# Four modulation steps in the router's wait, and routing weights by a single f32r pass whose parts ScalarE adds

## The chip, the core and the metric

The kernel runs on one core of a Trainium2 chip. Its engines are TensorE (PE; its weight loads are listed as PEld), VectorE (DVE), ScalarE (ACT), GpSimd (POOL) and SyncE (SP), which issues nearly all DMAs here. The metric is the device time of one launch in microseconds; lower is better.

## The reference

A diffusion backbone of two layers over 256 latent and 256 context tokens of width 1024. Layer 0 mixes tokens by windowed attention, layer 1 by differential attention; a mixture of experts follows each. Layer 0's mixture works on all 512 tokens, layer 1's on the 256 latent ones. What the change touches is the modulation `mod`, one row of 6 x 1024 numbers per layer and token kind, and the weights of the experts:

```python
mod  = (silu(c)     @ mod_w[i] + mod_b[i]).reshape(B, 6, 1, D)
modc = (silu(c_ctx) @ mod_w[i] + mod_b[i]).reshape(6, D)
h = rmsnorm(x, norm_g[i, 0]) * (1 + mod[:, 1]) + mod[:, 0]
...
gsel = argmax(lg); p_grp = max(softmax(lg))          # one of 4 groups
top_p, top_i = top_k(softmax(le_sel), 2)             # two of its 8 experts
wts = p_grp * top_p / sum(top_p)
out[token] += wts * ((silu(u[:, :512]) * u[:, 512:]) @ w_down[e]),  u = h[token] @ w_up[e]
```

## The kernel before

**Loads.** All large weights come through one ordered list, `plan`, in pieces of 512 KB. SP issues them one after another, each into one of 43 slots of SBUF (`Slot`); a slot comes free when its last reader is done, and SP waits at the next load until there is a free one.

**Stages.** Projections of layer 0 to 114 us; windowed attention to 228; output projection to 283; the router of layer 0 to 300.4; its 16 expert pairs to 812; the attention of layer 1 to 1046; its router to 1062; its expert pairs to 1525; the end.

**Modulation steps.** `mod_step` (its products are L370) multiplies a quarter of the rows of a third of `mod_w` by the two condition vectors: four pieces of weights, eight products of 32 x 512 in f32, each two instructions on PE. They add up in one PSUM bank over four steps; the fourth returns `mod_finish`, which copies the sum to SBUF, turns it by four transposes (L385) and adds the biases. Of 12 steps four are done in the projections and eight in the attention, where the loop over units (head pair, part) calls one after the units in `MODS`. The last four give the first third of layer 1's modulation, which nothing in layer 0 reads. In the attention the Tile scheduler orders PE's work, so a step can be split there. A head pair has three units; the third's scores are L760, its transposes L792.

**Router (`moe`).** From the logits DVE finds group, two experts and `Mb`, the table of chosen experts (L1013). PE counts with it (L1018, L1024). DVE makes the places `key`, and from these each pair of experts gets `P`, a matrix of 512 tokens x 128 places that holds ones and zeros, in f32r. Meanwhile `shift` rounds the tokens of tiles 2 and 3 to two f32r parts, `hi` by ACT (L977) and `lo` by DVE (L978). In the first pair a pass over `P` gathers 1/rms (`ri`, L1142, copied by L1143). From the router on PE's order is as written in the code.

**Expert pair.** `gather` for pair p+1 runs inside pair p. `gather_weights` (L1188) multiplies `P` by three columns of `WR` (the weights of both experts and 1/rms; two columns in layer 1 and in the first pair) in f32, two instructions per tile, and DVE copies the columns out of PSUM (L1191 twice, L1193). `half` (L1152) gathers the tokens; its sum is scaled by 1/rms in layer 0 (L1162 on ACT, L1160 on DVE). `P` is turned (L1168). `spread_tokens` (L1198, L1200) turns the gathered tokens. `up` is L1209, `down` L1252, `gate` L1216 to L1218, `combine` L1291 with the residual additions L509 on DVE. The bank group G, of two PSUM banks, serves the weights' sums, the gathered halves and the turned `P` in turn.

Of the kernel before, what the change touches and what calls it, by code (L numbers as in the profile page):

```python
# [36 lines left out]
CAP = 64  # L37
# [7 lines left out]
MODS = range(0, 24, 3)  # L45
# [11 lines left out]
def _hybrid_dit(ctx, tc, a, out):  # L57
# [6 lines left out]
               for c, dt in (("f", F32), ("r", F32R))] for i in range(SLOTS)]  # L64
    const = ctx.enter_context(tc.tile_pool(name="const", bufs=1))
# [238 lines left out]
    ident2 = const.tile([128, 64], F32, name="ident2")  # L304
# [3 lines left out]
    ident_b = const.tile([128, 128], BF, name="ident_b")  # L308
# [10 lines left out]
    for t, op in enumerate((OP.is_gt, OP.is_lt)):  # L319
        m = const.tile([128, 128], BF, name=f"mask_b{t}")  # L320
# [58 lines left out]
    def mod_finish(l, third, halves, hb, acc):  # L379
        h0, nh = halves[0], len(halves)  # L380
        sb = row("q")
        ve.tensor_copy(sb[hb], acc[hb])
        tp = bank("G")
# [449 lines left out]
    tmp.free()  # L833
    rooms.pop().free()
# [21 lines left out]
    class Post:  # L856
        def __init__(self, l, nt, lb=None):
# [23 lines left out]
            homes[l].slot.free()  # L881
# [99 lines left out]

    def moe(l, nt, post, after, finish):
        T = nt * 128
        with tc.manual_schedule(engines=PE):
            lg = post.logits()
        post.shift(2, ge)
# [38 lines left out]
        WR = const.tile([128, nt, NE // 2, 3], F32, name=f"WR{l}", tag="WR")  # L1025
        W = WR[:, :, :, 0:2]
        cmi = const.tile([128, 1], I32, name=f"cmi{l}", tag="cmi")

        def weights():
# [22 lines left out]
            if not unit:  # L1052
                ve.tensor_copy(WR[:, :, :, 2], post.ri.unsqueeze(2).to_broadcast([128, nt, NE // 2]))
        h_slots, tok, unit = post.slots, post.tok, post.nr == 1

        np_ = NE // 2
        prev = st = None
        early_ks = range(0, KT // 2) if T == 512 else ()
        late_ks = range(len(early_ks), KT)
        for p in range(np_):  # L1060
# [17 lines left out]
            if p == IF_AT:  # L1078
# [6 lines left out]
                with tc.If(most > CAP):  # L1085
                    overflow(l, nt, key, W, None if unit else post.ri, tok, [hs_[k // 2].f(2, 512)[:, k % 2] for k in range(KT)])
# [39 lines left out]
    def gather(l, nt, p, key, WR, tok, unit, early=None, between=None, ri=None):  # L1126
# [56 lines left out]

    def gather_weights(P, WR, p, st, n):
        wps = bank("G")
        nt = P.shape[1]
        for t in range(nt):
# [617 lines left out]
```

## Time and profile before

| | us |
|---|---|
| median of 3 runs | 1551.51 (1550.75 to 1552.95) |
| the profiled execution | 1550.44 |
| its span, first to last instruction | 1548.8 |
| PE busy in it | 1458.1 (94%) |
| DVE, ACT, POOL busy | 655.5, 384.6, 184.2 |
| mean granted clock of PE | 0.981 |

Starts are microseconds from the span's begin. A granted clock of 1.00 is 2.4 GHz, of 0.50 is 1.2 GHz. Busy shares are means over stages; each stage has its own limit. "[8.10 <-DVE Mb L1013]" behind an instruction says how long its engine had been idle and which instruction ended that.

### The profile page before, as it was taken

Reading aid. Unit: us, or ns where it says so; the run is one execution under the profiler, and the core shown is the slowest. Engines: PE = TensorE matmul, PEld = TensorE weight load, DVE = VectorE, ACT = ScalarE, POOL = GpSimd, SP = SyncE. Lnnn points to the kernel's source line nnn. Section 1 sums busy time; section 2 is a strip of 40 time slices with the busy share of each in tenths; the row PEclk is TensorE's granted clock in tenths of the full one; section 3 lists DMA queues with packets and bytes.
Section 4 is the critical chain, followed back from the end, with each engine's and each line's share of the span. In section 5 each row is a group of like instructions: output and inputs, shape, how many; then the busy total and the mean of one; then the engine's idle time right before and its main releaser. Section 6 shows DMA issues by size and latency. Waiting matters only on the chain. (4 is left out here: it accounts for less than half of the span.)

```text
span 1548.8 us, 20271 instructions
## 1 busy us (share of the span) xinstructions
PE 1458.1 (94%) x7463; PEld 800.3 (52%) x7463; DVE 655.5 (42%) x1585; ACT 384.6 (25%) x823; POOL 184.2 (12%) x147
## 2 busy tenths in 40 slices
PE   6998999799999999999999899798999899999997
PEld 4765567445444454444545678684434333433444
DVE  3338862424333443333448726863323222322323
ACT  4426653211010011101115235652101010110112
POOL 2314551000000000000006463100000000000000
PEclk9999999899999999999998999999999999999999
DMA  9767225799989999999996532488999999999991
GB/s 330 243 214 273 82 86 187 278 366 401 395 343 393 401 398 398 391 397 403 382 297 229 182 124 71 161 284 304 387 409 409 409 408 409 409 409 409 409 394 68
DMA packets 169695, 485.67 MB, mean 314 GB/s; under 512 B 20825, under 2 KB 41586, under 8 KB 169586
## 3 DMA queue, kind: packets, MB, share of 16 engines
q1 hardware_dynamic: 169088, 483.66, 82.2%
q8 instruction: 63, 1.03, 0.3%
q10 hardware_dynamic: 498, 0.60, 0.1%
q14 instruction: 46, 0.38, 0.1%
HBM read 483.16 MB, written 1.05 MB: 313 GB/s over the span
## 5 line engine op out<-in xcount | busy, mean ns | idle before, releaser
L1209 PE MATMUL ps<-slotf,row 128*64 128x512 f32 x2048 | 449.2, 593 | 2.1 <-DVE row L1200 2.1
L1209 PEld LDWEIGHTS ps<-slotf,row 128*64 128x64 f32 x2048 | 145.2, 137 | 289.7 <-issue 274.4
L1252 PE MATMUL ps<-slotf,row 128*64 128x512 f32 x960 | 212.6, 595 | 0.0
L546 PE MATMUL ps<-slotr,slotr 128*128 128x512 f32 x768 | 193.4, 405 | 13.4 <-DVE slotf L1414 6.7
L509 DVE SCALAR_TENSOR_TENSOR slotf<-ps,mod,slotf 128x256 f32<-128x256 f32 x408 | 167.3, 477 | 62.3 <-PE ps L1291 29.7
L546 PEld LDWEIGHTS ps<-slotr,slotr 128*128 128x128 f32 x768 | 145.1, 194 | 50.4 <-DVE slotf L1414 7.1
L1252 PEld LDWEIGHTS ps<-slotf,row 128*64 128x64 f32 x960 | 66.3, 137 | 124.9 <-issue 118.9
L1216 ACT ACTIVATE row<-ps 128x512 f32<-128x512 f32 x30 | 17.9, 597 | 425.9 <-PE ps L1209 386.6
L1217 DVE SCALAR_TENSOR_TENSOR row<-row,ps 128x512 f32<-128x512 f32 x30 | 20.6, 687 | 234.4 <-ACT row L1216 234.3
L1278 DVE SCALAR_TENSOR_TENSOR row<-ps,ty,row 128x512 fp32r<-128x512 f32 x60 | 45.0, 750 | 176.5 <-ACT row L1277 173.3
L1277 ACT ACTIVATE row<-ps,ty 128x512 fp32r<-128x512 f32 x60 | 41.3, 688 | 263.0 <-PE ps L1252 262.7
L1291 PE MATMUL ps<-row,row 128*128 128x512 f32 (+1 forms) x512 | 104.4, 348 | 1.1 <-DVE slotf L509 1.0
L1291 PEld LDWEIGHTS ps<-row,row 128*128 128x128 f32 x512 | 77.3, 189 | 36.5 <-ACT row L1216 21.1
L521 POOL TENSOR_TENSOR slotr<-slotf,slotr 128x1024 fp32r<-128x1024 f32 x32 | 78.9, 2479 | 86.9 <-ACT slotr L517 72.1
L1200 DVE TENSOR_TENSOR row<-ps,mod 128x512 f32<-128x512 f32 x64 | 42.7, 686 | 101.7 <-PE ps L1198 100.9
L481 POOL TENSOR_TENSOR row<-row,row 128x512 f32<-128x512 f32 (+1 forms) x13 | 15.0, 1156 | 575.6 <-PE ps L1291 519.4
L1152 PE MATMUL ps<-slotf,row 128*128 128x512 f32 x128 | 65.0, 632 | 7.0 <-PEq L1085 4.7
L1152 PE MATMUL ps<-slotr,row 128*128 128x512 f32 x256 | 70.4, 419 | 0.0
L517 ACT ACTIVATE slotr<-slotf 128x1024 fp32r<-128x1024 f32 x44 | 45.9, 1055 | 63.1 <-DMA slotf<-in_diff_w_qkv 38.0
L1152 PEld LDWEIGHTS ps<-slotr,row 128*128 128x128 f32 x256 | 47.9, 198 | 10.0 <-issue 0.8
L1377 PE MATMUL ps<-slotr,slotr 128*128 128x512 f32 x192 | 47.6, 399 | 0.0
L1198 PE MATMUL ps<-ident,row 128*128 128x128 f32 x256 | 37.8, 280 | 7.5 <-DVE row L1156 6.7
(314 smaller groups left out, 1526.8 us busy)
## 6 DMA issues: line engine op xcount, KB each, us to landing
slotf<-in_moe_w_up SPq DMA_DIRECT2D x512, 512.0 KB, 9.5
slotf<-in_moe_w_down SPq DMA_DIRECT2D x256, 512.0 KB, 10.2
slotf<-in_mod_w SPq DMA_DIRECT2D x96, 512.0 KB, 6.3
slotf<-in_diff_w_qkv SPq DMA_DIRECT2D x24, 512.0 KB, 3.9
slotf<-in_win_w_qkv SPq DMA_DIRECT2D x12, 512.0 KB, 5.2
slotf<-in_win_w_o SPq DMA_DIRECT2D x8, 512.0 KB, 4.0
slotf<-in_diff_w_o SPq DMA_DIRECT2D x8, 512.0 KB, 4.1
slotf<-in_x SPq DMA_DIRECT2D x2, 512.0 KB, 4.1
```

What stands on the lines that cost most here:

```text
L509: ve.scalar_tensor_tensor(xT[k][:, sl], ps[:, sl], g[:, k, r:r + 1], xT[k][:, sl], op0=OP.mult, op1=OP.add)
L517: se.activation(hv, v, AF.Copy)
L521: (eng or (ge if split_i[0] % 3 == 0 else ve)).tensor_tensor(lv, v, hv.bitcast(F32), op=OP.subtract)
L546: pe.matmul(ps[t], h[:, x, ts], w[y][:, kk, :], start=(k + kk == 0 and n == 0), stop=(k + kk == KT - 1 and n == 2))
L1152: pe.matmul(g, P[:, t, :] if len(tok[t]) > 1 else P[:, t, :].bitcast(F32), v[:, hs], start=(t == 0 and i == 0), stop=(t == nt - 1 and i == ...
L1200: ve.tensor_tensor(o.rearrange("p (k c) -> p k c", k=4), ps.rearrange("p (k c) -> p k c", k=4), mods[l][:, 3, 4 * h:4 * h + 4, 0:1].to_bro ...
L1209: pe.matmul(u[h][64 * s:64 * s + 64, :], st["xt"][k // 4][:, c0:c0 + 64], w[s][1][:, h * 512:(h + 1) * 512], start=(k == 0), stop=(k == KT ...
L1252: pe.matmul(y[h][64 * s:64 * s + 64, :], acT[:, c0:c0 + 64], w[s][1][:, h * 512:(h + 1) * 512], start=(k == 0), stop=(k == 3))
L1277: se.activation(yh, y[h], AF.Copy, scale=wsl)
L1278: ve.scalar_tensor_tensor(yl, y[h], wsl, yh.bitcast(F32), op0=OP.mult, op1=OP.subtract)
L1291: pe.matmul(out, part[:, c * 128:(c + 1) * 128], st["PT"][:, :T], start=(i == 0), stop=(i == 1))
L1377: pe.matmul(ps, w[x][:, k % 4, ms], oT0[k][1][:, y, :], start=(k == 0 and i == 0), stop=(k == KT - 1 and i == 2))
```

## The change

Three things, all in one file. `MODS` names every sixth unit instead of every third, so four of the eight steps leave the attention. Three of the four are put behind the transposes of layer 0's logits (`mods_meanwhile`); the fourth behind the counts (`last_mods`), its sum copied by ACT and turned after the first gather; the loads of these four steps stand behind those of the output projection. The weights' table `WR` becomes f32r in two parts, hi and lo, and the pass over it f32r by f32r, one instruction per tile over both parts' columns; the parts are added by an ACT copy with an accumulator output (`add_parts`), in place of DVE's copies. The same is done for 1/rms (`rr`). The constants of the attention's masks go into a slot that is freed after it, which pays for the larger `WR`.

```diff
-MODS = range(0, 24, 3)
+MODS = range(0, 24, 6)
...
+    while len(todo) > KT // 2:
+        plan_mod(*todo.pop(0))
+    plan_out(a["win_w_o"][0])
     while todo:
         plan_mod(*todo.pop(0))
-    plan_out(a["win_w_o"][0])
...
-    ident2 = const.tile([128, 64], F32, name="ident2")
+    masks = Slot()
+    ident2 = masks.f()[:, 0:64]
...
+    def mods_meanwhile():
+        while len(mod_steps) > 1:
+            mod_step("A")
+
+    def last_mods():
+        l, third, halves, hb, acc = mod_step("A").args
+
+        def moved():
+            sb = row("q")
+            se.activation(sb[hb], acc[hb], AF.Copy)
+            return partial(mod_turned, l, third, halves, hb, sb)
+
+        return moved
...
             lg = post.logits()
+            mods_meanwhile()
...
-        WR = const.tile([128, nt, NE // 2, 3], F32, name=f"WR{l}", tag="WR")
-        W = WR[:, :, :, 0:2]
+        moved = last_mods() if mod_steps else None
+        cols = 2 if unit else 3
+        WR = const.tile([128, nt, NE // 2, 2, cols], F32R, name=f"WR{l}", tag="WR")
...
+        if not unit:
+            rr = const.tile([128, nt, 2], F32R, name=f"rr{l}")
+            ve.tensor_copy(rr[:, :, 0], post.ri)
+            ve.tensor_tensor(rr[:, :, 1], post.ri, rr[:, :, 0].bitcast(F32), op=OP.subtract)
...
+            hi, lo = WR[:, :, :, 0, :], WR[:, :, :, 1, :]
+            se.activation(hi, wide_w, AF.Copy)
+            ve.tensor_tensor(lo, wide_w, hi.bitcast(F32), op=OP.subtract)
...
+        turn_mods = moved() if moved else lambda: None
...
-                    st = gather(l, nt, 0, key, WR, tok, unit, weights, ri=post.ri)
+                    st = gather(l, nt, 0, key, WR, tok, unit, weights, ri=() if unit else rr)
+                    turn_mods()
...
-                    pe.matmul(wps[:, 0:1], P[:, t, :].bitcast(F32), ri[:, t:t + 1], start=(t == 0), stop=(t == nt - 1))
-                ve.tensor_copy(st["w"][:, 1:2], wps[:, 0:1])
+                    pe.matmul(wps[:, 0:2], P[:, t, :], ri[:, t, :], start=(t == 0), stop=(t == nt - 1))
+                add_parts(st["w"][:, 1:2], wps[:, 0:2])
...
+    def add_parts(dst, src):
+        n = src.shape[0]
+        se.activation(tiny("ap", [128, 2], bufs=2)[:n], src, AF.Copy, accum_out=dst)
+
     def gather_weights(P, WR, p, st, n):
...
+        c = WR.shape[4]
         for t in range(nt):
-            pe.matmul(wps[:, 0:n], P[:, t, :].bitcast(F32), WR[:, t, p, 0:n], start=(t == 0), stop=(t == nt - 1))
+            pe.matmul(wps[:, 0:2 * c], P[:, t, :], WR[:, t, p], start=(t == 0), stop=(t == nt - 1))
+        v = wps[:, 0:2 * c].rearrange("p (b c) -> p c b", b=2)
         for s in range(2):
             pb = slice(64 * s, 64 * s + 64)
-            ve.tensor_copy(st["w"][pb, 0:1], wps[pb, s:s + 1])
+            add_parts(st["w"][pb, 0:1], v[pb, s])
         if n == 3:
-            ve.tensor_copy(st["w"][:, 1:2], wps[:, 2:3])
+            add_parts(st["w"][:, 1:2], v[:, 2])
```

The change adds lines, so a line of before has another number after: L370 is 375, L748 is 756, L749 757, L785 793; in the router and the experts L977 is 987, L1018 1044, L1024 1050, L1142 1182, L1152 1192, L1162 1202, L1168 1208, L1188 1233, L1198 1244, L1200 1246, L1209 1255, L1216 1262, L1217 1263, L1218 1264, L1242 1288, L1291 1337, L509 517.

PE in the attention, from the transposes of a second unit's probabilities to the scores of the next one, before; L370 is the modulation step:

```order
L785 MATMUL ps_1308<-ident,row_1190 128x128 x4
L370 MATMUL ps_1058<-slotf_125,slotf_109 32x512
L785 MATMUL ps_1315<-ident,row_1191 128x128 x4
L370 MATMUL ps_1058<-slotf_127,slotf_109 32x512
L370 MATMUL ps_1058<-slotf_111,slotf_109 32x512
L370 MATMUL ps_1058<-slotf_69,slotf_109 32x512
L370 MATMUL ps_1058<-slotf_125,slotf_109 32x512
L370 MATMUL ps_1058<-slotf_127,slotf_109 32x512
L370 MATMUL ps_1058<-slotf_111,slotf_109 32x512
L370 MATMUL ps_1058<-slotf_69,slotf_109 32x512
L748 MATMUL ps_1334<-slotr_124,slotr_94 128x512 x2
```

The same engine after, in a head pair whose loop calls no step:

```order
L793 MATMUL ps_1481<-ident,row_1363 128x128 x4
L375 MATMUL ps_1097<-slotf_129,slotf_109 32x512
L793 MATMUL ps_1488<-ident,row_1364 128x128 x4
L756 MATMUL ps_1495<-slotr_90,slotr_132 128x512 x2
L757 LDWEIGHTS slotb_169
L757 MATMUL ps_1495<-slotb_169 128x128
```

Where eight products stood in every head pair, this one holds a single product, between the two transposes; the next head pair holds the other seven of the step, two and five.

PE in the router of layer 0 after, from the counts (L1050) to the first gathered half; `ps_2639` is the sum of the moved steps:

```order
L1050 LDWEIGHTS ones_b
L1050 MATMUL ps_2730<-Mb_2715,ones_b 128x32
L375 MATMUL ps_2639<-slotf_75,slotf_109 32x512
...
L375 MATMUL ps_2639<-slotf_67,slotf_109 32x512
L1182 MATMUL ps_2793<-rr_2748,row_2758 128x2 x4
L1192 MATMUL ps_2800<-slotr_120,row_2758 128x512
L1192 MATMUL ps_2800<-slotr_114,row_2758 128x512
```

Before, the pass over `ri` (L1142) followed the counts at once; now seven products of the fourth step (the first and the last are shown) stand between them, and 1/rms is passed in two columns. The fourth step's first product stands ahead of L1044, behind the 24 of the three other steps.

ACT in an expert pair of layer 0, from one pair's last scaling of outputs to the second half of the next gather; before:

```order
L1277 ACTIVATE row_2952<-ps_2923,ty_2728 128x512
L1216 ACTIVATE row_3036<-ps_2957 128x512
L1162 ACTIVATE row_3081<-ps_3072,ty_3063 128x512
L1170 ACTIVATE row_3088<-ps_3083 128x512
L1242 ACTIVATE row_3095<-ps_3090 128x512
```

After:

```order
L1323 ACTIVATE row_3002<-ps_2973,ty_2760 128x512
L1262 ACTIVATE row_3086<-ps_3007 128x512
L1226 ACTIVATE ty_3119,ty_3113<-ps_3114 64x2
L1226 ACTIVATE ty_3121,ty_3113<-ps_3114 64x2
L1226 ACTIVATE ty_3123,ty_3113<-ps_3114 128x2
L1202 ACTIVATE row_3134<-ps_3125,ty_3113 128x512
L1210 ACTIVATE row_3141<-ps_3136 128x512
L1288 ACTIVATE row_3148<-ps_3143 128x512
```

Three additions (L1226), which read the weights' sums `ps_3114`, stand between the gate's activation (L1262) and the scaling of the gathered half (L1202); DVE's two copies are gone from its queue.

## Rows read from the trace of the kernel before

**Rows 1.** Stretches: from:to, length; busy (count) PE, PEld, DVE, ACT, POOL; clock, DMA, GB/s.
```profile
283.00:300.40 17.40, 7.14 (x40) 5.71 (x39) 13.75 (x55) 5.23 (x10) 2.52 (x2) 0.61 0.69 266
300.40:812.00 511.60, 503.71 (x2443) 243.20 (x2444) 190.54 (x425) 61.44 (x102) 2.17 (x2) 0.99 0.98 380
```

**Rows 2.** Stretches: the attention's first one, and one head pair.
```profile
113.70:136.40 22.70, 17.85 (x117) 9.08 (x117) 21.45 (x58) 12.67 (x35) 8.79 (x8) 1.00 0.87 307
172.70:184.60 11.90, 11.90 (x87) 6.94 (x85) 10.74 (x28) 7.35 (x23) 7.18 (x6) 1.00 0.14 45
```

**Rows 3.** Timeline in that head pair: start, us, engine, line, operation, count [idle <-releaser].
```profile
176.38 1.21 PE L760 MATMUL ps<-slotr,slotr 128*128 128x256 f32 x8
179.96 1.04 PE L370 MATMUL ps<-slotf,slotf 128*32 128x512 f32 x2
181.53 1.92 PE L370 MATMUL ps<-slotf,slotf 128*32 128x512 f32 x14
182.09 2.04 POOL L789 TENSOR_TENSOR slotf<-slotf,ty 128x512 f32<-128x512 f32 x2 [2.23 <-DVE ty L770]
184.60 0.82 PE L792 MATMUL ps<-ident,slotf 128*128 128x128 f32 x6
```

**Rows 4.** Timeline of the router, layer 0; then a stretch of it.
```profile
291.02 0.18 PE L1018 MATMUL ps<-Mb,before_b 128*128 128x32 bf16 x1 [8.10 <-DVE Mb L1013]
292.65 1.84 PE L1142 MATMUL ps<-ri,row 128*128 128x1 f32 x8 [1.09 <-DVE s L1031]
293.30 0.63 ACT L977 ACTIVATE slotr<-slotf 128x512 fp32r<-128x512 f32 x1 [2.56 <-DVE slotf L974]
294.35 3.76 PE L1152 MATMUL ps<-slotr,row 128*128 128x512 f32 x8
294.52 0.16 DVE L1143 COPY ty<-ps 128x1 f32<-128x1 f32 x1 [0.99 <-PE ps L1142]
300.38 3.65 PE L1209 MATMUL ps<-slotf,row 128*64 128x512 f32 x16 [0.78 <-DVE row L1200]
...
291.00:298.05 7.05, 5.94 (x31) 4.98 (x31) 5.36 (x19) 1.46 (x4) 0.00 (x0) 0.50 0.40 136
```

**Rows 5.** Timeline of one expert pair of layer 0.
```profile
513.75 2.83 DVE L509 SCALAR_TENSOR_TENSOR slotf<-ps,mod,slotf 128x256 f32<-128x256 f32 x7
513.95 0.95 PE L1188 MATMUL ps<-WR,row 128*128 128x3 f32 x8
514.73 1.69 PEld L1152 LDWEIGHTS ps<-slotr,row 128*128 128x128 f32 x8
514.76 2.09 PE L1152 MATMUL ps<-slotr,row 128*128 128x512 f32 x8
516.83 0.16 DVE L1193 COPY ty<-ps 128x1 f32<-128x1 f32 x1
517.13 0.63 PE L1168 MATMUL ps<-ident,row 128*128 128x128 f32 x4 [0.28 <-DVE ty L1193]
```

**Rows 6.** Waits of PE in layer 0's experts: us, times, longest.
```profile
PE ps L1168 <- DVE ty L1193: 3.7, 13, 0.3
```

**Rows 7.** ACT's instructions by form: count, busy us, mean ns, idle before.
```profile
L768 ACT ACTIVATE ty<-ty 128x2 f32<-128x2 f32 x16 | 3.3, 205 | 0.0
L753 ACT ACTIVATION_READ_ACCUMULATOR row<-ps,ty 128x1 f32 x32 | 6.5, 203 | 0.0
```

**Rows 8.** Timeline of one expert pair of layer 1.
```profile
1265.52 0.50 PE L1188 MATMUL ps<-WR,row 128*128 128x2 f32 x4
1265.72 0.69 DVE L1156 COPY row<-ps 128x512 f32<-128x512 f32 x1 [2.12 <-PE ps L1152]
1266.47 1.09 PE L1198 MATMUL ps<-ident,row 128*128 128x128 f32 x8 [0.45 <-DVE row L1156]
```

**Rows 9.** Stretches: layer 0's steady pairs, layer 1's first pairs.
```profile
481.00:740.00 259.00, 256.69 (x1232) 124.86 (x1233) 98.34 (x220) 30.68 (x49) 0.00 (x0) 0.99 1.00 397
1095.00:1220.00 125.00, 122.86 (x594) 51.79 (x592) 34.14 (x71) 13.35 (x24) 0.00 (x0) 1.00 1.03 409
```

More of the change, by code (lines that the diff above doesn't have):

```diff
@@ L64, in _hybrid_dit @@
                for c, dt in (("f", F32), ("r", F32R))] for i in range(SLOTS)]
+    halves = [nc.alloc_sbuf_tensor_at(f"slotb{i}", [128, 2048], BF, offset=base + 4096 * i).ap() for i in range(SLOTS)]
     const = ctx.enter_context(tc.tile_pool(name="const", bufs=1))
@@ L303, in _hybrid_dit @@
     make_identity(nc, ident)
-    ident2 = const.tile([128, 64], F32, name="ident2")
+    masks = Slot()
+    ident2 = masks.f()[:, 0:64]
+    masks_b = halves[masks.s].rearrange("p (a n) -> p a n", n=128)
     ve.tensor_tensor(ident2, ident[:, 0:64], ident[:, 64:128], op=OP.add)
@@ L307, in _hybrid_dit @@
     ve.memset(ones, 1.0)
-    ident_b = const.tile([128, 128], BF, name="ident_b")
+    ident_b = masks_b[:, 8]
     ve.tensor_copy(ident_b, ident)
@@ L319, in _hybrid_dit @@
     for t, op in enumerate((OP.is_gt, OP.is_lt)):
-        m = const.tile([128, 128], BF, name=f"mask_b{t}")
+        m = masks_b[:, 9 + t]
         ve.tensor_scalar(m, diff_f, 0.0, -BIG, op0=op, op1=OP.mult)
@@ L379, in mod_finish, with mod_turned @@
     def mod_finish(l, third, halves, hb, acc):
-        h0, nh = halves[0], len(halves)
         sb = row("q")
         ve.tensor_copy(sb[hb], acc[hb])
+        mod_turned(l, third, halves, hb, sb)
+    def mod_turned(l, third, halves, hb, sb):
+        h0, nh = halves[0], len(halves)
         tp = bank("G")
@@ L833, in _hybrid_dit @@
     tmp.free()
+    masks.free()
     rooms.pop().free()
@@ L880, in __init__ @@
                 ve.tensor_tensor(self.ws[:, r], wr[l], scl[l][1][:, :, r:r + 1].to_broadcast([128, KT, 36]), op=OP.mult)
-            homes[l].slot.free()
+            if not mod_steps:
+                homes[l].slot.free()
             self.slots = [[Slot() for _ in range(1 if t in WHOLE[l] else 2)] for t in range(nt)]
@@ L1052, in weights @@
             if not unit:
[L1053 to L1054 removed]
+                ve.tensor_copy(wide_w[:, :, :, 2], post.ri.unsqueeze(2).to_broadcast([128, nt, NE // 2]))
+            hi, lo = WR[:, :, :, 0, :], WR[:, :, :, 1, :]
+            se.activation(hi, wide_w, AF.Copy)
+            ve.tensor_tensor(lo, wide_w, hi.bitcast(F32), op=OP.subtract)
+        h_slots, tok = post.slots, post.tok
         np_ = NE // 2
         prev = st = None
+        turn_mods = moved() if moved else lambda: None
         early_ks = range(0, KT // 2) if T == 512 else ()
@@ L1085, in moe @@
                 with tc.If(most > CAP):
-                    overflow(l, nt, key, W, None if unit else post.ri, tok, [hs_[k // 2].f(2, 512)[:, k % 2] for k in range(KT)])
+                    overflow(l, nt, key, WR, None if unit else post.ri, tok, [hs_[k // 2].f(2, 512)[:, k % 2] for k in range(KT)])
                 for s in hs_:
@@ L1090, in moe @@
                 if p == 0:
-                    st = gather(l, nt, 0, key, WR, tok, unit, weights, ri=post.ri)
+                    st = gather(l, nt, 0, key, WR, tok, unit, weights, ri=() if unit else rr)
+                    turn_mods()
+                    if moved:
+                        homes[l].slot.free()
                 if p != IF_AT:
@@ L1318, in overflow @@
         Wov = row("p", (128, nt, NE))
-        ve.scalar_tensor_tensor(Wov.rearrange("p t (a b) -> p t a b", b=2),
-                                key.rearrange("p t (a b) -> p t a b", b=2), float(CAP), W,
+        pairs = Wov.rearrange("p t (a b) -> p t a b", b=2)
+        ve.tensor_tensor(pairs, W[:, :, :, 0, 0:2].bitcast(F32), W[:, :, :, 1, 0:2].bitcast(F32), op=OP.add)
+        ve.scalar_tensor_tensor(pairs, key.rearrange("p t (a b) -> p t a b", b=2), float(CAP), pairs,
                                 op0=OP.is_gt, op1=OP.mult)
```

3 lines of the change are left out of this document (added).

## The prediction

> **What bounds the kernel now.** I read the stages first, then inside each stage the wait that ends last. In the experts of layer 0 TensorE (PE) is busy 503.71 of 511.60 us [rows 1]: an instruction less there is time less, and an idle gap there is time too. The router ahead of them is the opposite: 7.14 busy of 17.40 us. PE stands 8.10 us for `Mb`, the table of chosen experts that VectorE (DVE) makes, and what follows runs at a granted clock of 0.50, the 1.2 GHz level [rows 1, 4]. In the windowed attention a head pair takes 11.90 us with PE busy throughout, while the first stretch is DVE's: 21.45 of 22.70 us against PE's 17.85 [rows 2]. So modulation steps cost PE time in the attention and would find an idle PE in the router; but PE being full in the attention doesn't yet say that its work is what sets the period.
>
> The profiled execution is 1550.44 us, 1.1 under the median of 1551.51. I make the sum on it and add the 1.1.
>
> **Part 1: four steps leave the attention.** A step is 16 instructions of L370. They stand as 2 + 14: from 179.96 to the next start at 180.94 is 0.98 us, and the 14 last 1.85 beyond what they overlap, together 2.83 [rows 3]. Before, the first stretch holds two steps beside the last one of the projections, and each of the six head pairs behind it one. After, by the order of PE, the first stretch keeps one step and one product (of the eight; two instructions) of the next, and the six pairs hold in turn two and five products, one, two and five, one, two and five, none. Two and five cost 0.98 + 1.85 as before, one costs 0.98. So PE is spared 1.85 in the first stretch, 1.85 in two pairs and 2.83 in the last, 8.4 us in all: the most that can be won.
>
> What is late next is the head pair's own chain. The third score (L760) ends at 177.59, and its transposes (L792) start at 184.60: 7.0 us of maximum, exponentials, sum, reciprocal and a multiplication on GpSimd, whose 2.04 us began when DVE's reciprocal L770 let it and waited for nothing of PE [rows 3]. PE fills 2.83 of the 7.0 with the step; with one product it has 5.2 of work there, with none 4.2. The links follow one another on ACT, DVE and GpSimd, so I let a pair with one product shorten by 0.6 and not by 1.85, the pair with none by 1.0, and the first stretch, where DVE is the busier, by 0.8: **−3 us**. Bounds: −8.4 if the chain gives way, 0 if it is rigid.
>
> The new weights' order on the SP queue (the output projection's eight loads before the last four steps' 16) costs nothing: these 16 must wait for slots of the attention either way and then stand ready before the router. The masks now hold a slot until the attention ends, one of 43; 0 to +1, I take 0.
>
> **Part 2: the router takes them.** Three steps, 3 x 1.85 = 5.6 us, stand behind the logits' transposes and inside the 8.10 us in which PE waits for `Mb` [rows 4]: free, and if that cover were gone they would cost their 5.6. The fourth's first product stands with them; its other seven stand after the counts and ahead of the pass that reads 1/rms (L1142 before). PE would reach it at about 291.7 (two DVE operations more in front of `Mb` or behind it, 0.3) and leave it at 293.5 at full clock, 295.4 at half. L1142, eight instructions in 1.84 at half clock, becomes four: 0.9 or less. It ends at about 294.0 to 296.3; before it was 294.49. On ACT two things come between: the copy of the fourth step's sum (about 0.6) and the addition of the 1/rms parts (0.4), and behind them in the queue stands L977, the rounding of the last token tile, which before started at 293.30 [rows 4]. It starts 1.3 to 3 us later, and the second half of L1152 needs it. Against that, L1152 took 3.76 here and 2.09 at full clock [rows 4, 5], and DVE no longer stands 0.99 for L1142 at L1143. The first expert matmul started at 300.38; I get 299.5 with the clock at its upper level and 302.5 to 303 at the lower one, and take **+0.5** (−1 to +3), since three steps leave PE some 2.5 us idle ahead of `Mb` where it had 8.10. Turning the fourth sum (four transposes, five small DVE operations) lies beside the 0.78 us for which PE waits at L1209 anyway.
>
> **Part 3: the weights' pass in layer 0, 15 pairs.** L1188 starts at 513.95 and L1152 behind it at 514.76: 0.81 us for eight instructions of 3 columns, 0.10 each [rows 5]. After: four of 6 columns, single-pass. With so few columns the count sets the price: 0.40, so −0.41. Bounds: L1152's eight weight loads of the same type take 1.69, 0.21 each [rows 5]; at that price four cost 0.85, no gain. Then the wait: L1168 stands 0.28 for L1193, 3.7 us in 13 pairs [rows 6]. PSUM has two banks of this group, L1168 writes the one that the weights' sums are read from, and the copies L1191 and L1193 queue on DVE behind seven residual additions, 2.83 us [rows 5]. Now ACT empties the bank, and in the order nothing stands between its last activation of the pair before and the three additions. Each is an ACTIVATE of two columns and a read of the accumulator: 205 + 203 ns by their nearest rows [rows 7], a = 0.41. They start with the sums at about 514.5, end at 515.7, and L1168 wants the bank at 516.45. So the 0.28 is gone up to a = 0.65, and PE follows at once. 15 x 0.41 + 3.7 = **−9.9** (−3.7 to −11); the first pair's pass, outside these 15, adds **−0.4**.
>
> The rows say that DVE is late here by its queue and not by its price; so I take ACT. The Trainium skill, page "ScalarE: Activation LUTs", section "Rules for kernel authors", says the reverse for the operation as such: additions belong on VectorE. By that rule the 0.28 would stay and the sum would be 3.7 us less, 1542; [rows 5, 6] don't bear it out, the longer instruction stands in an empty queue.
>
> For the f32r weight loads I keep to the rows, 0.10 to 0.21 each. The Trainium skill, page "TensorE: Matmul & The Clock Gate", section "Weight-path perf modes — Fast Weight Load (FWL) and DoubleRow", has weights other than FP32 loaded about twice as fast; by it the pass would be some 0.2 and the sum 3 us lower, an estimate. The f32r loads of L1152 show nothing of that [rows 5].
>
> **Part 4: layer 1, 15 pairs.** Four instructions become two, but the pass lies under another wait: L1198 starts 0.45 after L1188's work, held by the DVE copy L1156 [rows 8]. Gain 0. Two additions on ACT instead of L1191 free the bank at 1265.8 + 2a = 1266.6; the second spread needs it at about 1266.95. **0**, with a loss of 2a − 1.15 a pair beyond a = 0.57; 0 to +2 in all.
>
> **DMA.** At −0.7 a pair layer 0 asks its 24 transfers of 512 KB per 31.07 us, 405 GB/s; it has 397 now and layer 1 shows 409 [rows 9]. It holds, by little: the floor is 30.8 us a pair.
>
> Sum: −3 + 0.5 − 9.9 − 0.4 = −12.8: 1537.6 on the profiled execution, **1538.7** on the median.
>
> **Rivals.**
> 1. The attention's chain gives way, since DVE and ACT get their input earlier: −8.4 instead of −3, 1533. For it: PE without a gap [rows 2]. Against: the 7.0 us chain.
> 2. The clock is low when the fourth step starts: it and L1152 run at 1.2 GHz, the router costs +3, and the attention gives 0 to −1: 1543. For it: 0.50 in this very stretch [rows 4].
> 3. The f32r pass costs what eight instructions did; only the wait goes: 1538.7 + 6.2 = 1545.
> 4. Slower: the additions on ACT hold the bank. If each takes 1 us, because the read waits until the sum has left the engine, layer 1 loses 2 − 1.15 = 0.85 a pair and layer 0 3 − 1.95 = 1.05: 15 x 1.9 = +28.5 against −12.8, 1567. It decides from a = 0.79, where 15 x (5a − 3.1) eats the 12.8. Against: 0.2 for the read in every row of [rows 7].
> 5. The steps' 16 slots stay held until the router, 8 MB of experts come 20 us later, and layer 0 starts without a lead; SP is then the bound, and the gain of the pairs goes to DMA: 1546 or more. Against: 397 of 409 GB/s leaves pairs able to catch up [rows 9], and the first expert weights are loaded before.
> 6. The steps do not move at all in time, because their weights arrive late in the router: then 5.6 us stand behind `Mb`: 1544. Inside 5's chance.
>
> **How the numbers follow.** Forecast 0.56, rival 1 0.10, rival 2 0.15, rival 3 0.09, rival 4 0.04, rivals 5 and 6 0.06. The range 1530 to 1546 takes in the forecast with its bounds and rivals 1 to 3; it leaves out rival 4 and most of 5, and mixed cases. About 0.2%, 3.1 us, is what a measurement of this kernel can tell from none: faster needs less than 1548.4, which all but 4 and the worse half of 5 give: 0.92 faster, 0.04 the same, 0.04 slower.
>
> **What would show it.** Right: pairs of layer 0 near 31.05 us with no wait of L1168 on the weights; the waits of L1198 in layer 1 unchanged; the three steps inside PE's wait for `Mb`; head pairs alternating 12 and 11.4. Wrong: a first expert matmul later than 303, read-accumulator rows far above 0.2, or SP waits on slots in layer 0 longer than before.

## The result, and the profile after

The changed kernel takes 1539.4 us (median of 4 runs, 1537.48 to 1542.93), the kernel before 1551.76 beside it (4 runs, 1550.75 to 1552.95): a ratio of 0.9923, 95% interval 0.9903 to 0.9943. The interval lies below 1, so it is faster, 0.7 us above the forecast of 1538.7 and inside the range. Runs of one kernel differ by up to 10 us here, so below parts are compared stage by stage, and small differences of whole times only where intervals part them.

The profiled execution is the one of 1537.48, with a span of 1535.8 where before had 1548.8, so 13.0 us are to be found. Read from the starts of the instructions that bound the stages:

| stretch | before | after | difference | predicted |
|---|---|---|---|---|
| to the first attention score | 115.53 | 113.79 | -1.74 | 0 |
| to the router's first transposes | 166.20 | 163.79 | -2.41 | -3 |
| to the first expert matmul | 18.65 | 17.18 | -1.47 | +0.5 |
| the first pair, to its gate | 16.96 | 16.97 | 0.0 | -0.4 |
| layer 0's pairs, first gate to last | 448.00 | 438.03 | -9.97 | -9.9 |
| to layer 1's first gate | 313.47 | 313.35 | -0.12 | 0 |
| layer 1's pairs | 413.00 | 415.66 | +2.66 | 0 to +2 |

**Layer 0's pairs.** The table's row ends at the first and the last gate of layer 0, and so holds 14 of the 15 pairs that the -9.9 is for. From the timelines, before and then after (start, us, engine, line, operation, count, idle time and what ended it):

```profile
317.34 0.60 ACT L1216 ACTIVATE row<-ps 128x512 f32<-128x512 f32 x1 [17.96 <-PE ps L1209]
765.34 0.60 ACT L1216 ACTIVATE row<-ps 128x512 f32<-128x512 f32 x1 [14.77 <-PE ps L1209]
```

```profile
311.73 0.60 ACT L1262 ACTIVATE row<-ps 128x512 f32<-128x512 f32 x1 [6.05 <-PE ps L1255]
749.76 0.60 ACT L1262 ACTIVATE row<-ps 128x512 f32<-128x512 f32 x1 [14.77 <-PE ps L1255]
```

An ordinary pair went from 31.76 to 31.10 us. One of them in the timeline of after, which answers to [rows 5]:

```profile
503.41 2.83 DVE L517 SCALAR_TENSOR_TENSOR slotf<-ps,mod,slotf 128x256 f32<-128x256 f32 x7
503.61 0.51 PE L1233 MATMUL ps<-WR,row 128*128 128x6 f32 x4
503.97 2.09 PE L1192 MATMUL ps<-slotr,row 128*128 128x512 f32 x8
504.15 0.17 ACT L1226 ACTIVATE ty<-ps 64x2 f32<-64x2 f32 x1 [2.62 <-PE ps L1233]
505.02 0.20 ACT L1226 ACTIVATION_READ_ACCUMULATOR ty<-ps 128x1 f32 x1
505.90 0.60 PE L1208 MATMUL ps<-ident,row 128*128 128x128 f32 x4
```

The pass takes 0.36 us from its start to that of L1192, where it took 0.81. DVE still has its seven residual additions, but ACT was idle and starts the three sums at 504.15; the last is read at 505.22, so one costs 0.36. L1208 wants the bank at 505.90 and no longer waits (before 0.28, [rows 5, 6]), as the prediction had it for L1168, its line before.

DMA held, as far as it could. Steady pairs of layer 0, in the form of [rows 9], and the waits of SP's queue in the experts of layer 0 (us, times, longest), before and then after:

```profile
300.00:460.00 160.00, 159.56 (x764) 74.66 (x763) 56.07 (x112) 23.93 (x64) 0.00 (x0) 1.00 1.03 409
```

```profile
SPq L177 <- DMA slotf<-in_moe_w_up: 129.0, 158, 2.0
SPq L177 <- PE ps L1252: 125.6, 62, 9.5
```

```profile
SPq L178 <- DMA slotf<-in_moe_w_up: 211.1, 237, 1.8
SPq L178 <- PE ps L1298: 8.3, 16, 2.1
```

SP now waits for DMA and hardly for slots: the loads run at 409 GB/s throughout. PE is still busy 159.56 of 160, so PE sets the 31.10 us; the floor of 30.8 that the prediction worked out from 409 GB/s is 0.3 away.

**The router.** This answers to [rows 4]: first the timeline of after, then the whole stretch.

```profile
278.70 6.20 PE L375 MATMUL ps<-slotf,slotf 128*32 128x512 f32 x50
286.38 0.18 PE L1044 MATMUL ps<-Mb,before_b 128*128 128x32 bf16 x1 [1.48 <-DVE Mb L1039]
286.81 1.92 PE L375 MATMUL ps<-slotf,slotf 128*32 128x512 f32 x14
288.66 0.60 PE L1182 MATMUL ps<-rr,row 128*128 128x2 f32 x4
288.84 0.60 ACT L1001 ACTIVATE row<-ps 128x512 f32<-128x512 f32 x1 [2.74 <-PE ps L375]
289.12 1.86 PE L1192 MATMUL ps<-slotr,row 128*128 128x512 f32 x7
289.48 0.63 ACT L987 ACTIVATE slotr<-slotf 128x512 fp32r<-128x512 f32 x1
291.68 0.50 PE L1192 MATMUL ps<-slotr,row 128*128 128x512 f32 x1 [0.69 <-DVE slotf L984]
294.76 3.65 PE L1255 MATMUL ps<-slotf,row 128*64 128x512 f32 x16 [0.60 <-DVE row L1246]
...
277.58:294.76 17.18, 14.01 (x111) 6.76 (x111) 14.59 (x63) 6.26 (x15) 2.55 (x2) 1.00 1.00 395
```

Three steps and one product stand in the wait for `Mb`, which shrinks from 8.10 to 1.48, and the other seven behind the counts. The granted clock stays 1.00, the 2.4 GHz level, where it was 0.50 from 291 on.

**Layer 1.** One pair, which answers to [rows 8]:

```profile
1252.13 0.69 DVE L1196 COPY row<-ps 128x512 f32<-128x512 f32 x1 [2.13 <-PE ps L1192]
1252.24 0.17 ACT L1226 ACTIVATE ty<-ps 64x2 f32<-64x2 f32 x1 [1.43 <-PE ps L1233]
1252.69 0.20 ACT L1226 ACTIVATION_READ_ACCUMULATOR ty<-ps 64x1 f32 x1
1252.94 1.09 PE L1244 MATMUL ps<-ident,row 128*128 128x128 f32 x8 [0.74 <-ACT ty L1226]
```

The two sums end at 1252.89 and now release the first of the two spreads (the first of these eight transposes), where DVE's copy of the tokens did (it ends at 1252.82 here). The price is 0.07 us a pair: 29.18 before, 29.25 after.

### The profile page after: what moved, and what is told of

It is laid out like the page before. It is cut to its first block, busy times and chain, and to the rows that moved or that the text cites. A ratio compares the mean times of both kernels' runs of the same rounds, so it can differ in the third digit from the quotient of the medians.

```text
span 1535.8 us, 20164 instructions
## 1 busy us (share of the span) xinstructions
PE 1445.9 (94%) x7363; PEld 788.0 (51%) x7363; DVE 644.0 (42%) x1508; ACT 410.3 (27%) x986; POOL 185.1 (12%) x147
## 5 line engine op out<-in xcount | busy, mean ns | idle before, releaser
L1262 ACT ACTIVATE row<-ps 128x512 f32<-128x512 f32 x30 | 17.9, 597 | 402.1 <-PE ps L1255 362.9
L1246 DVE TENSOR_TENSOR row<-ps,mod 128x512 f32<-128x512 f32 x64 | 42.7, 687 | 104.9 <-PE ps L1244 104.9
L1192 PE MATMUL ps<-slotf,row 128*128 128x512 f32 x128 | 65.5, 636 | 6.9 <-PEq L1122 4.7
L1192 PE MATMUL ps<-slotr,row 128*128 128x512 f32 x256 | 69.3, 413 | 0.7 <-DVE slotf L984 0.7
L1192 PEld LDWEIGHTS ps<-slotr,row 128*128 128x128 f32 x256 | 46.3, 191 | 13.6 <-ACT row L1202 2.8
L1244 PE MATMUL ps<-ident,row 128*128 128x128 f32 x256 | 38.3, 282 | 11.9 <-ACT ty L1226 11.2
```

The lines of the kernel that those rows point to most:

```text
L1192: pe.matmul(g, P[:, t, :] if len(tok[t]) > 1 else P[:, t, :].bitcast(F32), v[:, hs], start=(t == 0 and i == 0), stop=(t == nt - 1 and i == ...
L1244: pe.transpose(ps[:, k * 128:(k + 1) * 128], st["x"][h][:, k * 128:(k + 1) * 128], ident)
L1246: ve.tensor_tensor(o.rearrange("p (k c) -> p k c", k=4), ps.rearrange("p (k c) -> p k c", k=4), mods[l][:, 3, 4 * h:4 * h + 4, 0:1].to_bro ...
```

## The experiments

Periods are those of ordinary pairs, "router" is the stretch from its first transposes to the first expert matmul. Each ratio is to the kernel before on the same chip.

**1 and 2: each half alone.** The first moves the steps and keeps the f32 pass with DVE's copies; the second keeps the steps in the attention and takes the f32r pass with ACT's sums.

```
 e1_mods_only    MODS, the plan, mods_meanwhile and last_mods of the change; nothing else
 e2_f32r_only    the change with
-MODS = range(0, 24, 6)
+MODS = range(0, 24, 3)                  # and the order of loads of before
```

> The kernel before with only the four modulation steps moved: three ahead of Mb, the fourth behind the counts, their loads behind the output projection's; the weights' pass stays f32 in two instructions and DVE copies its columns. Theory (the parts of the change add up by stage, each as the trace of the whole change shows it): the router's first transposes at 277.6 instead of 281.7 (attention -4.1), the first expert matmul at 294.8 to 295.3 instead of 300.4 (router -1.0 to -1.5, since the pass over 1/rms keeps eight instructions), pairs of layer 0 unchanged at 31.76, layer 1 unchanged at 29.18: 1546.3, 5.3 less than before. Rival (the router's gain comes from the four-instruction f32r pass over 1/rms and from DVE not waiting for it): only the attention's 4, 1547.7 or more.

Measured: 1547.4 (9 runs), 0.9976 (0.9966 to 0.9986). Router 17.18 at a clock of 1.00; periods 31.76 and 29.18, as before. From the first score to the router 164.07. The theory's figures for the router and the pairs hold; the router's first transposes stand at 278.90, 2.8 earlier than before and not 4.1. By the ratio the whole is 3.7 us less than before (2.2 to 5.3), which does not part the theory (5.3) from the rival (4 or less): the rival falls by the router's length alone.

> The change without the move: MODS every third unit and the loads in the order of before; f32r parts of the weights and of 1/rms, added by ACT, as in the change. Theory: attention and first expert matmul where they were (300.4, within 0.6), pairs of layer 0 at 31.10 instead of 31.76 (-10.0), layer 1 29.25 instead of 29.18 (+1.1): 1542.8, 8.9 less than before. Rival (the pairs of layer 0 are shorter because the expert weights come earlier, now that the moved steps' loads stand elsewhere): pairs between 31.4 and 31.76, 1546 or more.

Measured: 1546.04 (6 runs), 0.9955 (0.994 to 0.9971). Periods 31.10 and 29.25, those of the whole change; the ordinary pairs are as expected and the time is 3 us more. In its profile that lies in several places: the first expert matmul comes at 301.21, 0.8 later than before, layer 0's pairs from first gate to last are 8.4 shorter and not 10, and from there to layer 1's first gate it takes 315.45, 2.0 more than before. Its router, without the steps, stays at a low clock, and is yet 0.8 shorter than before (18.65):

```profile
283.38:301.21 17.83, 8.13 (x42) 6.48 (x43) 14.76 (x63) 5.98 (x14) 2.53 (x2) 0.62 0.74 291
```

So in the router the f32r pass with ACT's sums brings 0.8 alone, the steps 1.5 alone, and the two together 1.5. By their ratios the halves bring 0.24% and 0.45%, 0.69% together; the whole brings 0.77% (0.57 to 0.97). They add up within the interval.

**3 and 4: the pass and its adding apart.** The change with the parts added by DVE, and the kernel before with its three sums copied by ACT.

```
 e3_dve_add     def add_parts(dst, src):
-        se.activation(tiny("ap", [128, 2], bufs=2)[:n], src, AF.Copy, accum_out=dst)
+        ve.tensor_reduce(dst, src, axis=AX.X, op=OP.add)
 e4_act_copy    the kernel before, three times
-            ve.tensor_copy(st["w"][pb, 0:1], wps[pb, s:s + 1])
+            se.activation(st["w"][pb, 0:1], wps[pb, s:s + 1], AF.Copy)
```

> The change with the parts added by DVE (a sum along the two columns) instead of by ACT; all else as in the change. Theory (in layer 0 the transposes of P wait for the bank that DVE empties behind its seven residual additions, and these end at the same time whether the pass before the gather is long or short): the pass is shorter by 0.4 but L1208 waits 0.65 to 0.75 for DVE, the pairs of layer 0 are back at 31.70 to 31.85, so the whole 10 us of layer 0 are lost; layer 1 has its 29.18 again (-1.1): 1548 against 1539.4 of the change. Rival (pass and wait are two separate gains): pairs at 31.38, the 0.28 back and the 0.38 kept: 1542.5.

Measured: 1548.84 (11 runs), 0.998 (0.9971 to 0.999). Layer 0's period is 31.79. Its timeline, and PE's wait in the experts of layer 0 (us, times, longest):

```profile
508.85 0.49 DVE L1225 TENSOR_REDUCE ty<-ps 64x1 f32<-64x2 f32 x3
509.49 0.63 PE L1208 MATMUL ps<-ident,row 128*128 128x128 f32 x4 [0.73 <-DVE ty L1225]
...
PE ps L1208 <- DVE ty L1225: 8.6, 12, 0.7
```

DVE's three reductions take 0.49 us in all, ACT's sums 1.07. They still lose, since they come behind the residual additions: the turned `P` is held up 0.73 us, and the cheaper pass is given back whole.

> The kernel before with the three (in layer 1 two) copies of the weights' columns on ACT instead of DVE; the pass stays f32 in eight instructions, nothing is moved. Theory: ACT is free there, so the 0.28 us wait of L1168 goes and nothing else does: pairs of layer 0 at 31.48, layer 1 at 29.18 to 29.25 (two copies of about 0.2 each end before the bank is wanted): 1547.6, 3.9 less than before. Rival (the wait only moves to the next bank or to the scaling on ACT): pairs at 31.7, 1551.

Measured: 1549.65 (12 runs), 0.9985 (0.9975 to 0.9995). Period 31.52, and no wait of L1168 is left. The whole is 2.3 us less than before by the ratio (0.8 to 3.9), where 3.9 was expected; 14 pairs at 0.24 are 3.4, and in this profile the router's first transposes come 2.2 later than before (283.89). So the four periods of layer 0 are:

| | DVE empties the bank | ACT empties it |
|---|---|---|
| f32 pass | 31.76 | 31.52 |
| f32r pass | 31.79 | 31.10 |

Alone the parts bring -0.24 and +0.03, together -0.66.

**5: the price of ACT's sums.** The change with each sum made twice.

```
 e5_adds_twice
+        for _ in range(2):
             se.activation(tiny("ap", [128, 2], bufs=2)[:n], src, AF.Copy, accum_out=dst)
```

> The change with each addition on ACT done twice, one after the other into the same place. Six of them hold the bank of layer 0 for about 2.1 us instead of 1.07, four that of layer 1 for 1.35 instead of 0.65. Theory (the additions are free until the gathered half ends, 0.68 us of slack in layer 0; in layer 1 none is left): pairs of layer 0 at 31.10 + 1.05 - 0.68 = 31.45 to 31.55, pairs of layer 1 at 29.25 + 0.65 = 29.9; first expert matmul later by 0.3 or so: 1539.4 + 6 + 10 = 1555, slower than before. Rival (a bank that ACT holds costs nothing, since PE has other work in its queue): pairs as in the change, 31.10 and 29.25, 1539.4.

Measured: 1544.06 (7 runs), 0.9966 (0.9953 to 0.9978). Periods 31.27 and 29.46, +0.17 and +0.21, less than expected. The waits, layer 0 and then layer 1:

```profile
509.51 0.66 PE L1208 MATMUL ps<-ident,row 128*128 128x128 f32 x4 [0.18 <-ACT ty L1227]
...
1257.43 0.42 PEld L1245 LDWEIGHTS ps<-ident,row 128*128 128x128 f32 x4 [0.35 <-ACT ty L1227]
```

The expectation took too little slack. In layer 0 the prediction's own limit is near: the sums have 3 x 0.65 = 1.95 us, and six took 2.05 (507.41 to 509.46), 0.1 too much, with a wait of 0.18. In layer 1 four took 1.35; the prediction's formula gives 1.35 - 1.15 = 0.20 over the kernel before, and the period is 0.28 over it (29.46 against 29.18). So ACT's sums do hold the bank, as the fourth rival said, but one costs 0.36 and not 1.

**6: layer 1's sums earlier.** The pass over `P` ahead of the second half, so that ACT has 2 us more.

```
 e6_pass_first    in gather
+            if unit:
+                gather_weights(P, WR, p, st, 2)
             half(1)
```

> The change with one move in layer 1: the pass over the weights stands ahead of the second gathered half instead of behind it, as in layer 0. Then its bank is empty before that half ends, the first spread can start at once in that bank, and only the second spread waits for DVE's copy of the half. Theory (in layer 1 the transposes of both spreads wait about 0.75 us for a bank, though the first one's data are ready): the first four transposes, 0.5 us, go into that wait, pairs of layer 1 at 28.75 to 28.85 instead of 29.25: 1539.4 - 6.5 = 1533. Rival (DVE's or ACT's copies of the tokens set the start of both spreads, or the DMA floor of layer 1's loads does): pairs at 29.2, 1539.

Measured: 1539.06 (6 runs), 0.992 (0.9903 to 0.9937). Layer 1's period is 29.02, 0.23 less; 0.4 to 0.5 was expected. The pass no longer lies under a wait:

```profile
1253.08 0.38 PE L1233 MATMUL ps<-WR,row 128*128 128x4 f32 x2
1255.18 0.60 PE L1244 MATMUL ps<-ident,row 128*128 128x128 f32 x4
1256.13 0.66 PE L1244 MATMUL ps<-ident,row 128*128 128x128 f32 x4 [0.35 <-DVE row L1196]
```

It had stood between the half and PE's wait, where it cost nothing; now its 0.28 (1253.08 to the second half at 1253.36) is on the path, and of the wait 0.35 remains, for DVE's copy of the half instead of ACT's sums. By whole times this kernel can't be told from the change (0.9923).

**7 and 10: all four steps ahead of the counts,** alone and with the edit of 6.

```
 e7_four_first, e10_both
-        while len(mod_steps) > 1:
-            mod_step("A")
+        done = None
+        while mod_steps:
+            done = mod_step("A")
+        return done
...
```

> The change with all four steps ahead of Mb; nothing between the counts and the pass over 1/rms. Theory: the wait for Mb takes the last seven products too but for 0.3, and 1.85 us leave the path behind the counts, where the chain then runs through DVE's P (ready 0.8 earlier than PE is in the change): from the router's first transposes to the first expert matmul 16.4 instead of 17.2, 1538.6. Rival (that chain is ACT's and DVE's, not PE's): 17.0 to 17.5, 1539.4.

Measured: 1540.4 (6 runs), 0.9934 (0.9919 to 0.9948). The router took 18.98, not less than 17.18: its clock was low before the steps began.

```profile
277.85:283.85 6.00, 6.00 (x32) 2.65 (x36) 5.46 (x33) 2.45 (x5) 1.27 (x1) 0.52 1.02 406
```

> The change with both: all four steps ahead of Mb, and in layer 1 the pass ahead of the second half. Theory: the sum of the two, 1532. Rivals: as in the two alone.

Measured: 1536.15 (6 runs), 0.9912 (0.9892 to 0.9931). Here the clock stayed up and the router took 16.49, 0.69 less than the change's and near the 16.4 of 7's theory; layer 1's period is 29.02 again. Of the 4 us above the expected 1532 some 3 are layer 1's pairs, which won 0.2 less each than was expected in 6.

```profile
277.08:293.57 16.49, 13.07 (x110) 6.65 (x111) 14.62 (x63) 6.37 (x15) 2.57 (x2) 1.00 1.02 408
```

**11 and 13: another bank for layer 1's pass,** with the edit of 7 and alone. The weights' sums go to group C, so that the two spreads have both banks of G.

```
 e11_bank_c, e13_bank_c_only
-            gather_weights(P, WR, p, st, 2)
+            gather_weights(P, WR, p, st, 2, "C")
...
-    def gather_weights(P, WR, p, st, n):
-        wps = bank("G")
+    def gather_weights(P, WR, p, st, n, tag="G"):
+        wps = bank(tag)
```

> All four steps ahead of Mb, and in layer 1 the pass over the weights again behind the second half but into a bank of group C instead of G, so that the first spread takes the bank that the turned P has left. Theory (both the pass and the first spread then lie under DVE's copy of the second half): pairs of layer 1 at 28.75 to 28.85, against 29.02 where the pass stood ahead of the half and 29.25 in the change; 3 to 4 less than that kernel's 1536.2 - that is 1532.5. Rival (the loads of layer 1 come at 409 GB/s, 30.8 us a pair, and the lead that they bring along is used up): pairs at 28.8 at first and above 30 at the end, 1536 or more.

Measured: 1533.21 (4 runs), 0.9886 (0.9871 to 0.9901). Layer 1's period is 28.73, 0.52 less than the change's and 0.45 less than before, and stays so to the last pair: the rival, that the loads then set the pace, is out. The second spread waits for the tokens again, 0.15 us:

```profile
1254.29 0.69 DVE L1198 COPY row<-ps 128x512 f32<-128x512 f32 x1 [2.13 <-PE ps L1194]
1255.04 0.66 PE L1246 MATMUL ps<-ident,row 128*128 128x128 f32 x4 [0.15 <-DVE row L1198]
```

> The change with only the bank of layer 1's weights' pass changed, from group G to C; the router as in the change (three steps ahead of Mb, the fourth behind the counts). Theory (the bank is worth 0.52 a pair in layer 1, 7.8 in all, whatever the router does): pairs of layer 1 at 28.73, layer 0 at 31.10, 1539.4 - 7.5 = 1532. It also says what four steps ahead of Mb are worth where TensorE's clock may fall ahead of them: if they are worth 0.7, this kernel is 0.7 slower than the one with both (1533.2); rival (the seven products behind the counts shelter the clock of what follows them): it is faster by 1 or more.

Measured: **1531.65** (6 runs, 1529.18 to 1537.01), **0.9883** (0.9866 to 0.9901), the best here; layer 1's period 28.74. Its router took 18.83, again with a clock that fell before the steps, so three steps ahead (17.18 at full clock, 18.83 after a fall) and four (16.49, 18.98, 19.02) cannot be told apart by whole times.

**12: work alone, and the clock.** The kernel before with 24 products behind the logits, which nothing reads: as much work as three steps, without moving any.

```
 e12_idle_work    after lg = post.logits(), in layer 0
+            for i in range(24):
...
+                pe.matmul(ps[32*j:32*j+32, :], ones[:, 0:32], post.db.f()[:, 0:512], start=True, stop=True)
```

> The kernel before with 24 needless products (32 x 512, f32, the form of a modulation step, into a bank that nobody reads) put on PE behind the logits' transposes of layer 0's router; 5.6 us of PE work more, nothing left out, nothing moved. Theory (the moved steps shorten the router by keeping PE's clock at its upper level; each kernel with steps there has had a granted clock of 1.00 in the router or fallen before it, each without them 0.62 or 0.63): from the router's first transposes to the first expert matmul 17.0 to 17.3 us at a clock of 1.00 instead of 18.65 at 0.63; 1.4 less than before in all, 1549.5 to 1550. Rival (the router's gain is the shorter pass over 1/rms and the copies on ACT): 18.6 or more, 1551 or slower.

Measured: 1553.48 (11 runs), 1.002 (1.0011 to 1.0029): slower. Router 18.67, as before.

```profile
291.69 0.18 PE L1023 MATMUL ps<-Mb,before_b 128*128 128x32 bf16 x1 [2.83 <-DVE Mb L1018]
...
283.50:288.86 5.36, 5.36 (x49) 1.53 (x49) 4.57 (x26) 1.96 (x3) 1.27 (x1) 1.00 1.02 407
293.00:298.50 5.50, 5.19 (x16) 4.41 (x17) 3.88 (x16) 1.46 (x4) 0.00 (x0) 0.50 0.10 30
```

The products run at 1.00, PE then stands 2.83 for `Mb`, and what follows from 293.00 on runs at 0.50. So "three steps' work keeps the clock up" falls as it was stated. In experiment 1 the idle time was 1.65, and seven products stood behind the counts; experiment 10 had none behind the counts, 0.64 of idle time ahead of them, and a clock of 1.00 too. Whether the shorter idle time alone makes the difference was not tried apart.

**9: what a head pair can win.** The change with the products of three of the attention's four steps left out.

```
 e9_no_steps    in mod_step
+            if l * 3 + third == 2 and k + 2 < KT: continue
...
```

> The change with the products of the first three of the four steps left out that remain in layer 0's attention (weights are still loaded and their slots freed; only the last of the four multiplies): the first stretch and four of the head pairs have no step on PE. Theory (a head pair's chain from its third score to its transposes sets the period once PE is not full): the two pairs that had two and five products go from 11.95 to 10.6 to 10.9, the two that had one stay at 10.6 to 10.9: from first score to the router's first transposes 163.8 - 2.3 = 161.5, or 160.5 with a gain in the first stretch. Rival (PE's work sets the period): the pairs at 9.1 to 9.9, 163.8 - 9.5 = 154.

Measured: one run, 1531.99; it leaves out products, so it is there for its timeline alone. From the first score to the router 160.99, 2.8 less than in the change, for some 8.5 us of PE work less (three times 2.83). PE now waits for the chain, in the timeline:

```profile
153.98 2.04 POOL L799 TENSOR_TENSOR slotf<-slotf,ty 128x512 f32<-128x512 f32 x2 [3.25 <-ACT slotf L806]
155.07 0.66 PE L802 MATMUL ps<-ident,slotf 128*128 128x128 f32 x4 [0.92 <-POOL slotf L799]
```

## Why the prediction held, and where its steps did not

**The sum** came out closer (13.0 against 12.8) than its parts. Ahead of the attention 1.7 us went that nothing forecast, and the router gave 2.0 more than its +0.5; against them the attention gave 0.6 less, the first pair 0.4 less, and layer 1 lost 2.7. That these cancel is luck.

**Layer 0's pairs, -9.9: right, and for its reason,** the one step that carries the result. 0.41 for the pass was 0.42 (31.52 to 31.10), and 0.28 for the wait 0.24 (31.76 to 31.52). Two terms added up is not the whole of it, though: the prediction never said what the 0.41 is worth if the wait stays. By experiment 3 it is worth nothing then, since PE reaches the bank sooner and waits longer. The third rival (a pass no cheaper) is out, and so is the fourth: a sum costs 0.36, not 1. The eleven ordinary pairs give 11 x 0.66 = 7.3 us; the first gives 0.4, the branch's pair 0.7 and the one behind it 1.6 (32.30 to 30.68). About 1 of this last is no part of the mechanism. In that pair PE waits 2.9 us for DVE, and behind the wait the granted clock differs. The pair before, and after:

```profile
478.97:511.27 32.30, 31.55 (x142) 16.04 (x144) 9.62 (x20) 3.76 (x7) 0.00 (x0) 0.89 0.99 389
```

```profile
470.25:500.93 30.68, 29.84 (x138) 14.37 (x140) 9.28 (x17) 4.75 (x12) 0.00 (x0) 0.94 1.03 408
```

Where its mean granted clock is 0.89 or 0.90 the pair takes 31.98 to 32.75 (before and seven experiments), at 0.94 or 0.95 it takes 30.64 to 31.15 (after and four), and at 1.00 it takes 29.41 (experiment 5). The mechanism's share of the row is about 9.0, and the seven other kernels with the same code in layer 0 took 438.05 to 439.64 for it, 8.4 to 10.0 less than before: that the row met -9.9 to the tenth is luck.

The rule weighed in the prediction, of the Trainium skill, page "ScalarE: Activation LUTs", section "Rules for kernel authors", that additions belong on VectorE, was tried by experiment 3. It holds for the price (0.49 us for DVE's three, 1.07 for ACT's) and not for this place: 31.79 us a pair against 31.10, because the queue ahead of the instruction costs more than the instruction. The prediction priced the rule too low, at 3.7 us (1542): experiment 3 took 1548.84, since with the shorter pass the wait is 0.73 and no longer 0.28. The faster loading of weights other than FP32 (the Trainium skill, page "TensorE: Matmul & The Clock Gate", section "Weight-path perf modes — Fast Weight Load (FWL) and DoubleRow") is not seen here for f32r: a load of `P` for the pass takes 0.19 us in after, as the f32 load did before, while the router's bf16 loads of the same 128 x 128 (L1044) take 0.10.

**The attention, -3: right in size.** Nine profiles with four steps there take 163.79 to 165.28 us from the first score to the router, eight of them at most 164.07; four with eight steps take 166.20 to 168.35. The 166.20 of before stands at a mean granted clock of 1.00 in this stretch; at the 0.99 of the eight, kernels with eight steps take 166.96 and 167.69 (experiments 4 and 2), about 3 to 4 more. The path to it was rougher. The chain behind the third score is shorter than the 7.0 us read: part of those was PE's own queue. In a pair with one product of after:

```profile
149.84 1.21 PE L768 MATMUL ps<-slotr,slotr 128*128 128x256 f32 x8
156.30 0.66 PE L800 MATMUL ps<-ident,slotf 128*128 128x128 f32 x4
157.30 0.66 PE L800 MATMUL ps<-ident,slotf 128*128 128x128 f32 x4 [0.34 <-POOL slotf L797]
...
147.20:158.00 10.80, 10.34 (x72) 6.59 (x74) 9.24 (x28) 7.26 (x24) 6.14 (x7) 1.00 0.00 1
158.00:169.94 11.94, 11.94 (x84) 6.94 (x86) 8.44 (x25) 7.26 (x23) 6.09 (x6) 1.00 0.09 25
```

From the third score's end at 151.05 to 156.30 it is 5.25. Pairs with one product took 10.80 and 10.93 where 11.4 was forecast, two of those with two and five 11.94. The last, with none, took 12.23 where it took 12.48 with a step before; a gain of 1.0 was forecast, but DVE is busy throughout there:

```profile
193.14:205.37 12.23, 9.90 (x70) 6.51 (x69) 12.23 (x37) 8.34 (x24) 6.13 (x6) 1.00 0.12 34
```

Two errors against each other left 0.6 of 3. The first rival, that the chain gives way by the whole 8.4, is out: the change won 2.4 of it, and experiment 9 takes away as much again and wins 2.8.

**The 1.7 us ahead of the attention** belong to no step of the sum. The first score starts between 112.24 and 116.93 in kernels that leave the projections as they are in after or before; four with eight steps start at 114.04 to 116.93, nine with four at 112.24 to 115.49. They overlap, though their means lie 1.5 apart, and no run here isolates a cause.

**The router, +0.5: wrong, -1.5 us,** in two terms. The prediction had -0.9 at the upper clock and +2 or more at the lower, and took a value between. The queue was priced for a low clock, which didn't come: L1152's gather took 2.09 at 2.4 GHz and 3.76 at 1.2 [rows 4, 5], and after has the upper level throughout. And L987 was taken to start 1.3 to 3 us later; it started at 289.48, right behind L1001 and 11.9 us behind the router's first transposes, where before it came 11.6 behind them. What its lateness costs is the 0.69 in which L1192's last instruction waits for tile 3 (L984). The second rival, a low clock when the fourth step starts, was not seen in any run. Where the clock fell earlier (experiments 7, 11 and 13), the router took 18.83 to 19.02, which is 0.2 to 0.4 above before and not 3.

**The first pair, -0.4: wrong, 0.0.** The pass is as much shorter as forecast, but it had covered something:

```profile
304.40 0.59 PE L1233 MATMUL ps<-WR,row 128*128 128x6 f32 x4
305.43 6.66 PE L1255 MATMUL ps<-slotf,row 128*64 128x512 f32 x30 [0.44 <-DVE row L1246]
```

PE now waits 0.44 for DVE's copy of the second spread (L1246), which had been ready under the longer pass. The step should have asked what is late next, as it did for the other pairs.

**Layer 1, 0 to +2: wrong, +2.7,** of which 0.07 a pair where the formula said nothing, and 1.6 in one pair. The formula's loss, 2a - 1.15, begins at a = 0.57, and two sums took 0.65 in all. It let the second spread need the sums' bank; in after it is the first spread that waits for it, and that one could start when DVE's copy ends, 0.07 ahead of the sums (in experiment 5 it is the second). About 1.0 us are the pairs. The rest stands in the pair behind the branch (28.16 before, 29.77 after), 1.09 of it in PE's timeline:

```profile
1220.62 0.49 PE L1286 MATMUL ps<-ident,row 128*128 128x128 f32 x3 [1.09 <-issue]
```

"issue" is time in which PE waited for nothing that the profile shows. Ten profiles have 0.9 to 1.7 us of it right there: after and eight experiments with the f32r pass, and experiment 12 with the f32 pass. Before and experiments 1 and 4, with the f32 pass, have none, nor has 9, with the f32r pass. So the pass isn't what makes it, and no run here shows what does: the cause is open. The remaining half microsecond goes with the granted clock of that pair, 0.94 before and 0.92 after; experiment 9, with 0.90 there and without the idle time, takes 29.38.

**DMA: right.** The loads run at 409 GB/s and not at 405, and PE was not held up. The fifth and sixth rivals did not come: SP's waits for slots fell from 125.6 to 8.3 us in the row shown.

## What to carry to other kernels

A shorter instruction is worth something only once what follows it is ready: before counting it, find the wait behind it and what that instruction covers, and move the late link too (here the two halves brought +0.03 and -0.24 alone and -0.66 together). Ask which engine has an empty queue at that moment before asking which is cheapest for the operation. And when two uses of one PSUM bank meet in a short loop, try another group first: that one word was worth 0.5 us a pair in layer 1, more than the pass's place in the order (0.23).

## What the hardware showed that was not expected

- The clock in the router hangs on more than the amount of work: 24 needless products and then 2.83 us of idle time left it at 0.50 behind the wait; with the moved steps and 0.64 to 1.65 us of idle time it was 1.00 in seven profiles, and in three it had fallen already when the steps began.
- A read of ACT's accumulator costs 0.20 us and the sum of two columns from PSUM 0.17, back to back 0.36 for a whole addition.
- A 128 x 128 weight load took 0.19 us in f32r as in f32, and 0.10 in bf16.
- PE stood 0.9 to 1.7 us for "issue" right behind a branch, in ten profiles and not in four.
- 512 KB loads ran at 409 GB/s through the 160 us shown without holding PE up, at a margin of 0.3 us in 31.1.
